# Joining attention items over heads and groups, and silu through tanh, in a hybrid decoder trunk

## The chip, the cores and the metric

The kernel runs on one core of one Trainium2 chip. The core has five engines that run their own instruction lists in order: TensorE (PE, matrix products, with its weight loads shown as PEld), VectorE (DVE), ScalarE (ACT), GpSimd (POOL) and SyncE (SP), which here only issues DMAs. The metric is the device time of one execution in microseconds (us), as the median of several runs; the kernel before took 1153.44 us (three runs, 1150.41 to 1153.8).

## The reference

One batch of 512 tokens, width 1024, goes through two layers. Layer 0 is a short gated convolution followed by a squared-ReLU MLP. Its output is normalised and projected once into a shared key and value side. Layer 1 is native sparse attention followed by another MLP. The part that matters here is the attention: 16 heads in 4 groups, head size 64, four query blocks of 128 tokens, a learned bias by distance, and three branches.

```python
# shared side, once
k_raw, v_raw, k_sel, v_sel, k_win, v_win = split(h @ w_kv)
k_cmp = silu(blocks(k_raw + pe_k) @ phi_k_w1) @ phi_k_w2    # 31 blocks of 32 tokens, stride 16
v_cmp = silu(blocks(v_raw + pe_v) @ phi_v_w1) @ phi_v_w2
# per query block and head
o_c = softmax(q k_cmp + bias) v_cmp        # compressed
o_s = softmax(q k_sel + bias) v_sel        # selected blocks: 16 of 8, so all causal ones
o_w = softmax(q k_win + bias) v_win        # window of 512: all causal keys
o   = gate0 * o_c + gate1 * o_s + gate2 * o_w
x   = x + o @ w_o
```

With 512 tokens there are 8 selection blocks and up to 16 may be chosen, so the second and third branch both run over all earlier keys.

## The kernel before

All matrix operands are split into a high and a low float16 part, and each product is three matmuls (`mm3`, L338 to L341: high by high, high by low, low by high). Weights come from HBM in pieces through SP's queue (`load_piece`, L147) and are split by ScalarE (`whi`) and VectorE (`wlo`) in `convert_piece` (L169), a few pieces ahead of use.

The attention stage lies in the block that starts at L598. First come the projections that every item needs (keys, values, gates, the queries of group 0; L860). Then two kinds of work are interleaved.

*Items* (L898 and L972). A `Full` item is one head of one group `g`, one query block `qb` and one branch `br`; it sees nk = 128, 256, 384 or 512 keys for qb 0 to 3. There are 128 of them. A `Cmp` item is the compressed branch of four heads of one group and one query block; there are 16. Each item has five steps, which are emitted for different items in one turn of the loop:
- st0: two logits matmuls into a bank "b" (two banks), a reduction on VectorE that adds the bias T and finds the maximum (L919), and the exponential on ScalarE, with a read of its sum (L922).
- st1, two items later: transposes of the probabilities into a bank "c" (two banks), copied to float16 as `at_ph` by ScalarE (L931).
- st2, three items later: VectorE forms the low part `at_pl` (L934).
- st3, four items later: three value matmuls per 128 keys into the bank "d" (L946 to L948). After the last head of a block VectorE scales by gate over sum, and GpSimd adds the parts of the three branches into the tile `o`.
- st4, six items later: `finish` (L879) transposes the finished output and splits it for the output projection.

A `Cmp` item does the same with plain additions, maxima and sums of VectorE (L990 to L1000), in tiles of its own (`c_s`, `c_p`, `c_ph`, `c_pl`).

*Background* (L1047) is a generator of matrix products that yields after every few matmuls: the raw compressed keys, the queries of group 1, `phi(0)` (the MLP of the compressed keys, with the silu at L793), the raw compressed values, `phi(1)`, the queries of groups 2 and 3, and, once groups 0 and 1 are done, the first half of the output projection. A turn of the loop gives it 1.7 yields for the first 64 items and 0.9 after (L1083); a yield is usually three matmuls. An item whose queries or compressed keys are missing forces the background on (L1071).

The order of items is set at L1045: full items of groups 0 and 1, compressed items of 0 and 1, full items of 2, compressed items of 2 and 3, full items of 3. Inside these rules the program's scheduler puts each engine's instructions into their final order, so that the lists differ a little from the order in which they are written. The bias tiles T (two buffers) are loaded by a DMA on ScalarE's queue (`load_T`, L619), a VectorE copy `Tc` of each sixteenth column behind it; the second half of a group's items starts the load for the next group.

## Time and profile before

| | us or share |
|---|---|
| median of the runs | 1153.44 |
| the profiled execution | 1151.28, its span 1149.5 |
| PE busy | 1106.0 (96%) |
| DVE busy | 837.8 (73%) |
| ACT busy | 582.7 (51%) |
| POOL busy | 162.2 (14%) |
| HBM over the span | 98 GB/s |

The profile is taken from one execution. A busy share counts the time between an instruction's start and end; TensorE's matmuls overlap, so that its share says little about how fast it could go. A row of a group of instructions has line, engine, operation, output and inputs, shape and count, then the busy time and the mean nanoseconds of one, then the idle time of the engine just before them with what ended it. A row of a table of windows has the stretch, its length, the busy time of each engine with its instructions in brackets, the share of TensorE's full clock, and the DMA engines' share and rate. A row of the timeline has start, length, engine, line, operation and shape.

### The profile page before, as it was taken

Reading aid. Unit: us, or ns where it says so; the run is one execution under the profiler, and the core shown is the slowest. Engines: PE = TensorE matmul, PEld = TensorE weight load, DVE = VectorE, ACT = ScalarE, POOL = GpSimd, SP = SyncE. Lnnn points to the kernel's source line nnn. Section 1 sums busy time; section 2 is a strip of 40 time slices with the busy share of each in tenths; the row PEclk is TensorE's granted clock in tenths of the full one; section 3 lists DMA queues with packets and bytes.
Section 4 is the critical chain, followed back from the end, with each engine's and each line's share of the span. In section 5 each row is a group of like instructions: output and inputs, shape, how many; then the busy total and the mean of one; then the engine's idle time right before and its main releaser. Section 6 shows DMA issues by size and latency. Waiting matters only on the chain.

```text
span 1149.5 us, 20386 instructions
## 1 busy us (share of the span) xinstructions
PE 1106.0 (96%) x7959; PEld 694.1 (60%) x7959; DVE 837.8 (73%) x1604; ACT 582.7 (51%) x983; POOL 162.2 (14%) x211
## 2 busy tenths in 40 slices
PE   9999999999999999999999899999999999999996
PEld 4444444447884458868466665765444688445885
DVE  4755557765897557988487898997985588754795
ACT  4523235345333444457679778676644534343452
POOL 0000000422000220000120023111132200022031
PEclk9999999999999999999999999999999999999998
DMA  6433235433433333314333530111643343330231
GB/s 208 130 92 110 92 111 174 119 93 93 127 98 108 109 110 107 97 55 122 110 79 99 143 94 19 57 38 38 186 126 99 88 126 110 104 99 19 75 92 74
DMA packets 149379, 115.76 MB, mean 101 GB/s; under 512 B 8612, under 2 KB 146564, under 8 KB 149284
## 3 DMA queue, kind: packets, MB, share of 16 engines
q1 hardware_dynamic: 146736, 109.47, 31.8%
q10 hardware_dynamic: 2260, 4.40, 1.3%
q8 instruction: 62, 1.02, 0.4%
q0 software_dynamic: 288, 0.61, 0.2%
q14 instruction: 33, 0.27, 0.1%
HBM read 110.22 MB, written 2.14 MB: 98 GB/s over the span
## 4 chain that ended last, share of the span: by engine, by line
PE 49%; DVE 20%; ACT 12%; issue 8%; POOL 6%; DMA 4%; SPq 0%; DVEq 0%; ACTq 0%; POOLq 0%
POOL ml_z L501 6%; PE a L340 4%; PE a L339 4%; PE a L341 4%; DVE wlo L183 4%; DMA wst<-mlp_w_dram 4%; ACT rh L502 3%; PE b L339 3%; PE b L340 3%; PE b L341 3%; PE c L341 3%; PE c L339 3%; PE c L340 3%; DVE wst L180 3%; DVE wlo L194 3%
## 5 line engine op out<-in xcount | busy, mean ns | idle before, releaser
L193 ACT ACTIVATE whi<-wst 128x1024 f16<-128x1024 f32 (+2 forms) x171 | 142.2, 857 | 128.3 <-PE b L340 40.0
L194 DVE SCALAR_TENSOR_TENSOR wlo<-wst,whi 128x1024 f16<-128x1024 f32 (+2 forms) x171 | 168.1, 990 | 47.3 <-ACT whi L193 47.1
L501 POOL TENSOR_TENSOR ml_z<-ml_z 128x256 f32<-128x256 f32 x128 | 101.1, 811 | 604.5 <-ACT ml_z L499 403.9
L182 ACT ACTIVATE whi<-wst 128x1792 f16<-128x1792 f32 x64 | 107.0, 1692 | 132.6 <-DVE wst L180 107.8
L341 PEld LDWEIGHTS <-wlo 128*128 128x128 f16 x1024 | 100.1, 98 | 109.3 <-DVE wlo L194 0.7
L339 PEld LDWEIGHTS <-whi 128*128 128x128 f16 x1024 | 100.4, 98 | 108.1 <-issue 3.7
L503 DVE TENSOR_TENSOR rl<-ml_z,rh 128x1792 f16<-128x1792 f32 x32 | 64.8, 2025 | 136.9 <-ACT rh L502 136.9
L340 PEld LDWEIGHTS <-whi 128*128 128x128 f16 x1024 | 100.2, 98 | 105.0 <-issue 1.7
L183 DVE SCALAR_TENSOR_TENSOR wlo<-wst,whi 128x1792 f16<-128x1792 f32 x64 | 129.8, 2033 | 3.6 <-ACT whi L182 3.6
L180 DVE TENSOR_TENSOR wst<-wst 128x256 f32<-128x256 f32 x256 | 105.9, 455 | 24.1 <-DMA wst<-mlp_w_dram 23.1
L502 ACT ACTIVATE rh<-ml_z 128x1792 f16<-128x1792 f32 x32 | 54.3, 1697 | 103.4 <-POOL ml_z L501 103.4
L550 PEld LDWEIGHTS <-wlo 128*128 128x128 f16 x896 | 88.1, 98 | 16.6 <-issue 5.1
L549 PEld LDWEIGHTS <-whi 128*128 128x128 f16 x896 | 88.1, 98 | 14.8 <-issue 3.9
L548 PEld LDWEIGHTS <-whi 128*128 128x128 f16 x896 | 88.2, 98 | 11.0
L499 ACT ACTIVATE ml_z<-ml_t 128x1024 f32<-128x1024 f32 x32 | 33.8, 1057 | 90.5 <-DVE ml_t L497 90.5
L341 PE MATMUL b<-xsh,wlo 128*128 128x512 f16 x208 | 78.8, 379 | 0.0
L340 PE MATMUL b<-xsl,whi 128*128 128x512 f16 x208 | 78.8, 379 | 0.0
L339 PE MATMUL b<-xsh,whi 128*128 128x512 f16 x208 | 78.7, 379 | 0.0
L922 ACT ACTIVATE at_p<-at_s,at_m 128x128 f32<-128x128 f32 (+3 forms) x128 | 71.3, 557 | 13.4 <-DVE at_m L919 13.0
L549 PE MATMUL a<-rl,whi 128*128 128x256 f16 x256 | 70.3, 275 | 4.6 <-DVE rl L503 4.6
L339 PE MATMUL c<-xsh,whi 128*128 128x512 f16 x192 | 72.8, 379 | 0.0
L340 PE MATMUL c<-xsl,whi 128*128 128x512 f16 x192 | 72.8, 379 | 0.0
(312 smaller groups left out, 2757.5 us busy)
## 6 DMA issues: line engine op xcount, KB each, us to landing
wst<-mlp_w_dram SPq DMA_DIRECT2D x256, 256.0 KB, 3.4
wst<-a_w_in_dram SPq DMA_DIRECT2D x18, 512.0 KB, 3.6
wst<-w_kv_dram SPq DMA_DIRECT2D x12, 512.0 KB, 3.7
T<-ext_d ACTq DMA_DIRECT2D x4, 1056.0 KB, 6.0
wst<-a_w_out_dram SPq DMA_DIRECT2D x8, 512.0 KB, 3.5
wst<-b_w_qg_dram SPq DMA_DIRECT2D x8, 512.0 KB, 4.3
wst<-b_w_o_dram SPq DMA_DIRECT2D x8, 512.0 KB, 3.5
wst<-a_w_in_dram SPq DMA_DIRECT2D x8, 384.0 KB, 5.5
```

The costliest lines, as they stand in the source:

```text
L180: DVE.tensor_tensor(b[:, :, o], b[:, :, x], b[:, :, y], op=e)
L182: ACT.activation(hi, b[:, :, 1:], AF.Copy, scale=sc)
L183: DVE.scalar_tensor_tensor(lo, b[:, :, 1:], sc, hi, op0=OP.mult, op1=OP.subtract)
L193: ACT.activation(hi[:, s:e], w, AF.Copy, scale=sc)
L194: DVE.scalar_tensor_tensor(lo[:, s:e], w, sc, hi[:, s:e], op0=OP.mult, op1=OP.subtract)
L339: PE.matmul(ps, w[0], xs[0], start=start, stop=False)
L340: PE.matmul(ps, w[0], xs[1], start=False, stop=False)
L341: PE.matmul(ps, w[1], xs[0], start=False, stop=stop)
L501: POOL.tensor_tensor(z[:, o], z[:, a], z[:, b], op=e)
L502: ACT.activation(rh[0][:, p], z[:, 1:8], AF.Copy)
L548: PE.matmul(acc7[i], wh, xh, start=c == 0 and not other, stop=False, skip_group_check=other)
L549: PE.matmul(acc7[i], wh, xl, start=False, stop=False, skip_group_check=other)
```

## The change

- A `Full` item now takes a tuple of heads: all four for query block 0, two for block 1, one for blocks 2 and 3, so that each item fills at most 512 columns. Logits, reductions and exponentials stay per head; transposes, the copy `at_ph`, the subtraction `at_pl` and the value matmuls run over the joined tile. 128 items become 88.
- A `Cmp` item takes the eight heads of two groups; its tiles come from `at_s`, `at_p`, `at_ph` and `at_pl`. 16 items become 8. `finish` can take two groups, and `add_parts` replaces the two places that add branches. The output tile `o` has six buffers, each for a pair of groups and one query block.
- The silu of `phi` is computed as v (1 + tanh(v/2)) / 2: the bias is copied twice, ScalarE applies tanh and adds one, VectorE multiplies.
- The background's yields now say what they cost, in us of TensorE (0.65, 0.33, 0.42, by default 0.1), and a turn gives 1.1 up to item 44 and 0.7 after; a wait for the output of groups 0 and 1 drops the credit.
- The loads of T for groups 1, 2 and 3 stand at items 11, 35 and 60; `Tc` is one tile for two groups. Tiles `vc_t` and `phi_hd` become `at_s` and `kr_hl`.

```diff
@@ load_T
-            c = ap.tile([128, 4, 32], F32, name="Tc", bufs=4)
-            DVE.tensor_copy(c, t[:, :, 0:512:16])
-            TC[g] = c
+            if g % 2 == 0:
+                TC[g // 2] = ap.tile([128, 2, 4, 32], F32, name="Tc", bufs=2)
+            DVE.tensor_copy(TC[g // 2][:, g % 2], t[:, :, 0:512:16])
@@ gated_pair (values: 0.33, phi: 0.42, out_proj: 0.65)
-                        yield
+                        yield 0.65
@@ phi
-                bcol = ap.tile([128, 1], F32, name="phi_b", bufs=2)
-                ACT.activation(bcol, ph[m][:, 124:125], AF.Copy, scale=1.0 / (SW * SK))
+                bias = ap.tile([128, 2], F32, name="phi_b", bufs=2)
+                ACT.activation(bias[:, 0:1], ph[m][:, 124:125], AF.Copy)
+                ACT.activation(bias[:, 1:2], ph[m][:, 124:125], AF.Copy, scale=0.5 / (SW * SK))
                 t = ap.tile([128, G, 31], F32, name="phi_t", bufs=2)
-                ACT.activation(t, ph[m][:, 0:124].rearrange("p (g j) -> p g j", g=4), AF.Silu,
-                               bias=bcol, scale=1.0 / (SW * SK))
-                split_to(hs[:, m, 0, :, 0:31], hs[:, m, 1, :, 0:31], t, SR)
+                v = ph[m][:, 0:124].rearrange("p (g j) -> p g j", g=4)
+                ACT.activation(t, v, AF.Tanh, bias=bias[:, 1:2], scale=0.5 / (SW * SK))
+                ACT.activation(t, t, AF.Identity, bias=ones)
+                DVE.scalar_tensor_tensor(t, v, bias[:, 0:1], t, op0=OP.add, op1=OP.mult)
+                split_to(hs[:, m, 0, :, 0:31], hs[:, m, 1, :, 0:31], t, 0.5 * SR / (SW * SK))
@@ add_parts, in place of add_part
+        def add_parts(g, n, qb, src, scale):
+            if (g // 2, qb) not in og:
+                og[g // 2, qb] = ap.tile([128, 2, 256], F32, name="o", bufs=6)
+            dst = og[g // 2, qb][:, g % 2:g % 2 + n].rearrange("p g (h d) -> p (g h) d", d=64)
...
+            t = ap.tile([128, 512], F32, name="o_t", bufs=1)[:, 0:nb * nh * 64].rearrange(
+                "p (b h d) -> p b h d", b=nb, d=64)
+            DVE.tensor_tensor(flat(t), flat(src), sc, op=OP.mult)
...
@@ Full.st0
-                q = Qs[g][:, h, qb * 128:(qb + 1) * 128]
-                PE.matmul(s[:, :nk], q, KD[:, br, 0, g, :nk], start=True, stop=False)
-                PE.matmul(s[:, :nk], q, KD[:, br, 1, g, :nk], start=False, stop=True)
+                for j, h in enumerate(self.heads):
+                    q = Qs[g][:, h, qb * 128:(qb + 1) * 128]
+                    o = s[:, j * nk:(j + 1) * nk]
+                    PE.matmul(o, q, KD[:, br, 0, g, :nk], start=True, stop=False)
+                    PE.matmul(o, q, KD[:, br, 1, g, :nk], start=False, stop=True)
...
+                for j, h in enumerate(self.heads):
+                    w = slice(j * nk, (j + 1) * nk)
+                    DVE.tensor_tensor_reduce(lg[:, w], s[:, w], TG[g][:, h, lo:lo - nk:-1], -1.0 / SL, 3e38,
+                                             OP.add, OP.min, mn[:, j:j + 1])
+                    ACT.activation(self.p[:, w], lg[:, w], AF.Exp, bias=mn[:, j:j + 1], scale=-1.0,
+                                   accum_out=l[:, br * 4 + h:br * 4 + h + 1])
@@ Full.st1, st2 (self.w = nk * len(heads))
-                for b in range(self.nb):
+                for b in range(self.w // 128):
                     PE.transpose(pt[:, b * 128:(b + 1) * 128], self.p[:, b * 128:(b + 1) * 128], ident)
-                ACT.activation(self.pt[0][:, :self.nk], self.ps, AF.Copy, scale=SP)
+                ACT.activation(self.pt[0], self.ps, AF.Copy, scale=SP)
@@ Cmp.st0
-                s = bank("b")[:, 0:128].rearrange("p (h n) -> p h n", h=4)
-                for h in range(4):
+                s = bank("b")[:, 0:256].rearrange("p (h n) -> p h n", h=8)
+                for j in range(8):
+                    g, h = 2 * gp + j // 4, j % 4
...
-                lg = ap.tile([128, 4, 32], F32, name="c_s", bufs=2)
+                lg = ftile("at_s", 3)[:, 0:256].rearrange("p (h n) -> p h n", h=8)
@@ items and loop
+        def heads_of(qb):
+            n = max(1, 4 >> qb) if qb < 2 else 1
+            return [tuple(range(h, h + n)) for h in range(0, 4, n)]
...
-        items = full(0) + full(1) + cmps(0) + cmps(1) + full(2) + cmps(2) + cmps(3) + full(3)
+        items = full(0) + full(1) + [Cmp(0, qb) for qb in range(4)] + full(2) + [Cmp(1, qb) for qb in range(4)]
+        items += full(3)
+        at_item = {11: lambda: load_T(1), 35: lambda: load_T(2), 60: lambda: load_T(3)}
...
-            credit += 1.7 if i < 64 else 0.9
-            while credit >= 1.0:
-                run_bg(1)
-                credit -= 1.0
+            credit += 1.1 if i < 44 else 0.7
+            while credit > 0.0:
+                u = next(bg, "end")
+                if u in ("wait", "end"):
+                    credit = 0.0
+                else:
+                    credit -= u or 0.1
```

More of the change, by code (lines that the diff above doesn't have):

```diff
@@ L701, in values @@
                     next(cv, None)
-                    yield
+                    yield 0.33
             drain(cv)
@@ L1007, in st1 @@
+                self.pt = [ap.tile([128, S], F16, name=n, bufs=3)[:, :self.w] for n in ("at_ph", "at_pl")]
+                self.ps = pt[:, :self.w]
                 ACT.activation(self.pt[0], self.ps, AF.Copy, scale=SP)
@@ L1012, in st3 @@
             def st3(self):
-                g, qb = self.g, self.qb
-                po = bank("e")[:, 0:256]
-                vc = [VC[:, i, g].rearrange("p h d -> p (h d)") for i in range(2)]
-                PE.matmul(po, self.pt[0], vc[0], start=True, stop=False)
-                PE.matmul(po, self.pt[0], vc[1], start=False, stop=False)
-                PE.matmul(po, self.pt[1], vc[0], start=False, stop=True)
-                rl = ap.tile([128, 4], F32, name="rlc", bufs=2)
+                g, qb, br = self.g, self.qb, self.br
@@ new lines, in st3 @@
+                k = keep[self.g, self.qb]
+                if k[0] is None:
+                    k[0] = bank("d")
+                vc = slice(br * 256 + g * 64, br * 256 + g * 64 + 64)
+                for j, h in enumerate(self.heads):
+                    o = k[0][:, (br * 4 + h) * 64:(br * 4 + h) * 64 + 64]
+                    for b in range(self.nb):
+                        at = j * self.nk + b * 128
+                        ph, pl = (u[:, at:at + 128] for u in self.pt)
+                        PE.matmul(o, ph, VT[:, b, 0, vc], start=b == 0, stop=False)
+                        PE.matmul(o, ph, VT[:, b, 1, vc], start=False, stop=False)
+                        PE.matmul(o, pl, VT[:, b, 0, vc], start=False, stop=b == self.nb - 1)
@@ new lines, in st3 @@
+                if self.heads[-1] == 3 and br == 1:
+                    rl = ap.tile([128, 8], F32, name="rl", bufs=2)
+                    by = rl.rearrange("p (b h) -> p b h", h=4)
+                    gt = GT[:, qb, 12 * g:12 * g + 12].rearrange("p (h b) -> p b h", b=3)[:, 1:3]
+                    DVE.reciprocal(rl, k[1])
+                    DVE.tensor_tensor(by, by, gt, op=OP.mult)
+                    add_parts(g, 1, qb, k[0].rearrange("p (b h d) -> p b h d", b=2, d=64), rl)
+                    self.last = parts[g, qb] == 2
+                else:
+                    self.last = False
@@ L1059, in body @@
         bg = background()
-        def run_bg(n):
-            for _ in range(n):
-                if next(bg, "end") in ("wait", "end"):
-                    return
         lead = {1: 2, 2: 3, 3: 4, 4: 6}
```

243 lines of the change are left out of this document (108 added, 135 removed).

## The prediction

> **What bounds the kernel now.** I read the busy shares by stage first, then the spacing of TensorE's instructions, then the groups of instructions. The attention items run from 559.5 to 796 us; before and after them TensorE is dense and the change issues nothing. The windows below cut that stage at the first item of each group (0, 1, then the compressed items of 0 and 1, group 2, compressed items of 2 and 3, group 3).
>
> ```profile
> span 1149.5 us, 20386 instructions
> ```
> ```profile
> core 0: us, PE busy (x) PEld busy (x) DVE busy (x) ACT busy (x) POOL busy (x), PEclk, DMA share, GB/s
> 559.50:613.90 54.40, 50.24 (x515) 34.54 (x514) 42.34 (x126) 42.84 (x115) 10.33 (x10) 1.00 0.32 90
> 613.90:676.30 62.40, 56.48 (x606) 37.79 (x605) 50.08 (x153) 51.06 (x142) 3.31 (x4) 1.00 0.37 104
> 676.30:691.10 14.80, 13.98 (x172) 9.28 (x171) 13.72 (x56) 8.83 (x23) 8.06 (x12) 1.00 0.38 112
> 691.10:735.60 44.50, 41.68 (x420) 27.86 (x418) 41.31 (x141) 36.20 (x112) 11.00 (x14) 1.00 0.12 37
> 735.60:748.60 13.00, 12.93 (x167) 9.06 (x165) 12.50 (x57) 6.93 (x21) 3.37 (x7) 1.00 0.14 42
> 748.60:796.00 47.40, 42.99 (x460) 29.39 (x461) 41.91 (x143) 34.93 (x110) 6.74 (x10) 1.00 0.12 35
> ```
>
> The stage takes 236.5 us. VectorE (DVE) sums to 201.9 in it and ScalarE (ACT) to 180.8, so neither is full. TensorE shows 218.3, but its records overlap, and what it needs is read from the spacing in a dense stretch of the timeline:
>
> ```profile
> 605.31 0.23 PE L341 MATMUL a<-big,wlo 128*128 128x155 f16 x1
> 605.38 0.60 PE L928 MATMUL c<-ident,at_p 128*128 128x128 f32 x4
> 605.82 0.19 PE L946 MATMUL d<-VT,at_ph 128*128 128x64 f16 x1
> ...
> 606.08 0.38 PE L914 MATMUL b<-KD,Q 128*128 128x512 f16 x1
> 606.30 0.38 PE L915 MATMUL b<-KD,Q 128*128 128x512 f16 x1
> ```
>
> A matmul of 155 columns takes 0.07 us, four transposes 0.44, the nine value matmuls between 605.82 and 606.08 take 0.029 each, one of 512 columns 0.216 (0.42 ns a column). The counts in the stage, grouped by shape:
>
> ```profile
> L928 PE MATMUL c<-ident,at_p 128*128 128x128 f32 x320 | 57.4, 279 | 6.1 <-DVE at_pl L934 5.4 <-ACT at_ph L931 0.2
> L946 PE MATMUL d<-VT,at_ph 128*128 128x64 f16 x320 | 43.5, 193 | 2.0 <-ACT at_ph L931 1.4 <-DVE o_t L957 0.3
> L341 PE MATMUL a<-xqh,wlo 128*128 128x512 f16 x48 | 18.2, 379 | 0.0
> L341 PE MATMUL a<-big,wlo 128*128 128x512 f16 x36 | 13.6, 379 | 0.0
> L341 PE MATMUL a<-big,wlo 128*128 128x155 f16 x64 | 13.6, 233 | 0.0
> L341 PE MATMUL a<-xsh,wlo 128*128 128x512 f16 x30 | 11.4, 379 | 0.0
> ```
>
> Each L341 stands for three matmuls. Background of 512 columns: 114 rows here and about 5 more, x3 x0.216 = 77; of 155 columns 64x3x0.07 = 13; transposes 320x0.11 = 35; value matmuls 3x320x0.029 = 28; logits, 32 items of each of four widths, two matmuls each, 64x(0.054+0.108+0.162+0.216) = 35; compressed items and final transposes about 14. Together some 203 us. So **TensorE's own work is 203 of the 236.5 us and bounds the stage; about 33 us are waits** for VectorE and ScalarE, mostly shorter than a record's tail and hence not all visible as idle time.
>
> Where are they? A full-attention item costs TensorE 0.31, 0.61, 0.91 or 1.22 us (query block 0 to 3). Next are the items (the reductions of L919, two records each) and then the background triples (L341) in three stretches:
>
> ```profile
> 632.10:648.20 16.10, 5.93 (x24) 1.00 0.57 152
> 691.10:708.60 17.50, 5.41 (x33) 1.00 0.11 32
> 776.80:787.80 11.00, 4.79 (x15) 1.00 0.17 49
> ```
> ```profile
> 632.10:648.20 16.10, 0.00 (x0) 0.00 (x0) 1.00 0.57 152
> 691.10:708.60 17.50, 3.39 (x9) 0.78 (x8) 1.00 0.11 32
> 776.80:787.80 11.00, 0.76 (x2) 0.20 (x2) 1.00 0.17 49
> ```
>
> First: 4 items of block 1 and 8 of block 2 need 9.7 us of TensorE and took 16.1, no background: 6.4 lost. Second: 8+8 small items 7.4, nine triples 5.9, transposes of finished outputs about 1.3: 2.9 lost. Third: seven items of block 3 8.5 and two triples 1.3: 1.2 lost, a pace of 1.57 us an item. **An item without background beside it runs at the pace of the VectorE/ScalarE handoffs, one with it at TensorE's.** These three hold 10.5 of the 33; the other 23 are spread, with the start of the stage and its last output among them.
>
> **The change part by part.** TensorE's work does not change: the same matmuls and transposes, in 96 items for 144.
>
> Joined full items. 32 copies and 32 subtractions of 128 columns become 8 of each at 512; 32 of 256 become 16 at 512. Reductions and exponentials stay one per head.
>
> ```profile
> L934 DVE SCALAR_TENSOR_TENSOR at_pl<-c,at_ph 128x128 f16<-128x128 f32 x32 | 8.9, 284 | 1.8 <-ACT at_ph L931 1.7
> L934 DVE SCALAR_TENSOR_TENSOR at_pl<-c,at_ph 128x256 f16<-128x256 f32 x32 | 13.2, 419 | 2.4 <-ACT at_ph L931 2.3
> L934 DVE SCALAR_TENSOR_TENSOR at_pl<-c,at_ph 128x512 f16<-128x512 f32 x32 | 21.8, 685 | 1.8 <-ACT at_ph L931 1.5
> L931 ACT ACTIVATE at_ph<-c 128x128 f16<-128x128 f32 x32 | 8.7, 273 | 2.1 <-PE c L928 1.9
> L931 ACT ACTIVATE at_ph<-c 128x256 f16<-128x256 f32 x32 | 12.0, 379 | 6.6 <-PE c L928 4.9 <-PE d L948 1.5
> L931 ACT ACTIVATE at_ph<-c 128x512 f16<-128x512 f32 x32 | 18.7, 586 | 5.9 <-PE c L928 5.8
> ```
>
> VectorE: 32x(0.284+0.419) = 22.5 becomes 24x0.685 = 16.4, 6.1 less. ScalarE: 20.9 becomes 14.1, 6.8 less.
>
> Compressed items, 16 to 8, each with twice the columns. A doubled instruction costs about 1.5 single ones (0.284 to 0.419), so two become one at a saving of a quarter. The two stretches of compressed items hold 13.72+12.50 = 26.2 us of VectorE, so about 6 less; ScalarE, a copy and an exponential an item, 2 less. Tiles at_s, at_p, at_ph now serve these items and the value conversion too, three buffers each: a wait could arise there. It holds at most the next item in the queue; I take it as nothing, since an item's at_s is free once its exponential has read it; the bound is one pace, 1.57, for each of 8 items, 12.6.
>
> Silu through tanh. Today each silu has its own table and the next exponential loads its own back:
>
> ```profile
> 656.20 1.28 ACT L793 ACT_TABLE_LOAD   x1
> 657.50 0.36 ACT L793 ACTIVATE phi_t<-a,phi_b 128x124 f32<-128x124 f32 x1
> ```
> ```profile
> L922 ACT ACT_TABLE_LOAD x4 | 5.1, 1283 | 0.1
> L793 ACT ACT_TABLE_LOAD x3 | 3.8, 1283 | 0.1
> ```
>
> In the changed program's ScalarE list one load is left in the stage: 6x1.28 = 7.7 us less. Added are four more bias copies, four adds of one and four VectorE multiplications, all 124 columns or fewer: at most 0.36 each by the L793 row, under 3 us on ScalarE, 1.4 on VectorE. [...]
>
> So VectorE goes from 202 to about 191 and ScalarE from 181 to about 167. None of it shortens TensorE's 203; it is worth only what it takes off the 33 us of waits.
>
> Background. Each item now brings 1.1 us of background up to item 44 and 0.7 after, by its TensorE cost and not by count. For the joined blocks that is 1.1 us beside 1.22 us of item, for 0.31 to 0.61 before. The built program's order of TensorE shows where it lands. Without background stand: three items of block 1 at the head of group 1; the last nine of group 1 (one of block 2, eight of block 3), then the drain of the last of them, then the 96 matmuls of 155 columns in one piece; the last four of group 3. Group 2 has two to six background matmuls beside nearly every item. Cost: at the 1.57 pace against 1.22, nine items lose 3.1; the drain waits for a copy and a subtraction, 0.586+0.685, 1.3; three joined items lose about 0.5 each, since two reductions and a subtraction on VectorE (some 1.7 us) stand against 1.22, 1.5; the last four 1.4. That is 7.3 for 10.5: **3 us less**.
>
> The other 23 us come from handoffs. Two thirds of the items are left and both serving engines carry 6 to 8% less. Between waits that scale with load (23x0.07 = 1.6) and with items (23x0.33 = 7.7) I take 5: a joined item has one copy-subtract handoff instead of four or two, but its four exponentials still stand in the ScalarE queue ahead of the next copy. **Sum: 8 us less**, bounds 4.6 to 10.7 by these rows alone; below that, the buffer wait of 12.6 turns it into 5 to 8 more.
>
> The bias table's load (T) is issued at items 11, 35 and 60, at least nine items before its group; it lands in 6 us by the row below, nine items take over 9. It costs nothing; if it came late, the copy to Tc would hold VectorE's queue and with it every reduction.
>
> ```profile
> T<-ext_d ACTq DMA_DIRECT2D x4, 1056.0 KB, 6.0
> ```
>
> The profiled execution took 1151.28 us around its span of 1149.5, 2.2 below the runs' median of 1153.44. 1151.3-8 = 1143.3; for a median I add half that offset: **1144.5**.
>
> **The rivals.**
> (a) *The waits do scale with handoffs and the joined items hide fully behind their background.* Waits fall from 33 to about 19: 14 less, 1139. For it: group 2's 44.5 us against 40 of need, now covered. Against: ScalarE still does four exponentials and their reads per joined item.
> (b) *Nothing measurable.* The stage is TensorE's 203 plus waits that move: the block of 155-column matmuls and the rest of the q2 projection run while VectorE and ScalarE idle for some 10 us, and they make that up in groups 2 and 3, where VectorE is already at 41.3 of 44.5. 1150 to 1155. Against: even idle for 10 and then at the 0.93 of group 2, VectorE needs 191/0.93+10 = 215.
> (c) *Slower: the joined item's longer chain is exposed.* TensorE's value matmuls wait for copy and subtraction of all heads: (586-273)+(685-284) = 0.71 us longer on 8 items, (586-379)+(685-419) = 0.47 on 16, 13.3 in all, and a bank of logits is held until the last head's reduction. With the 3 us of cover still gained it ends at +10, 1162; it turns slower once over 60% of the 13.3 is exposed with nothing won on the handoffs. For it: TensorE already waits 5.4 us for at_pl (L928 row). Against: 1.1 us of background and another item's 1.22 now lie between.
> (d) [...] One row shows a lowered clock:
>
> ```profile
> 900.00:1000.00 100.00, 97.16 (x754) 75.03 (x753) 79.05 (x126) 38.48 (x29) 7.37 (x11) 0.97 0.37 111
> ```
>
> Three in a hundred of the clock are lost over these 100 us, 3 us. The stage's windows all have 1.00. [...]
> (e) *That the change doesn't do what it says:* excluded for the loads and the joins, which stand in the built instruction lists.
>
> **How the numbers follow.** Forecast 0.42 (with (d), which shares its time, 0.47), (a) 0.17, (b) 0.16, (c) 0.20. About 0.3%, 3.5 us, is what a measurement of this kernel can tell from no change. Faster is forecast, (d) and (a): 0.64; same (b) 0.16; slower (c) 0.20. The likeliest case alone spans 1140 to 1149; the range takes half of (a), all of (b) and the near part of (c): 1135 to 1158.
>
> **What would show it.** In the changed profile the stage should last about 228 us, with group 2 near 41 and group 1 about as long as now; TensorE's need still 203; VectorE near 191, ScalarE near 167; one table load. Waits of the transposes for at_pl should fall below their 5.4 us. A stage under 224 speaks for (a). If group 2 does not shorten, cover was not what it lacked. If the value matmuls' waits (L946 to L948 now) for at_ph or at_pl in blocks 0 and 1 grow to several us, (c) holds. A clock below 1.00 in the stage would be (d). A first item of any group waiting for POOL's part of Q or for T would be a step that I left out.

## The result and the profile after

| | median | lowest to highest | runs |
|---|---|---|---|
| before | 1152.80 us | 1150.41 to 1157.10 | 6 |
| after | 1143.95 us | 1143.17 to 1147.34 | 6 |

The ratio is 0.9925, with a 95% interval from 0.9903 to 0.9948. The changed kernel is 8.85 us faster; 1144.5 us was forecast.

The profiled execution of the changed kernel is its longest, 1147.34 us at a granted clock of 0.987; its five other executions had 0.992 to 0.994, and the profiled one of the kernel before had 0.994. So a second profiled execution of the same kernel, of 1143.29 us at 0.994, stands beside it below, called the second profile. The page of the first begins:

```profile
span 1145.5 us, 20148 instructions
## 1 busy us (share of the span) xinstructions
PE 1102.9 (96%) x7959; PEld 695.8 (61%) x7959; DVE 833.8 (73%) x1504; ACT 569.7 (50%) x925; POOL 152.8 (13%) x201
```

These are its stage windows, cut as in the prediction (groups 0 and 1, the compressed items of both, group 2, the compressed items of 2 and 3, group 3):

```profile
core 0: us, PE busy (x) PEld busy (x) DVE busy (x) ACT busy (x) POOL busy (x), PEclk, DMA share, GB/s
559.00:612.90 53.90, 50.22 (x483) 33.71 (x483) 41.58 (x115) 39.62 (x104) 10.25 (x10) 0.94 0.24 66
612.90:676.00 63.10, 55.99 (x655) 40.67 (x654) 50.81 (x146) 44.66 (x131) 3.18 (x5) 0.97 0.41 115
676.00:691.60 15.60, 12.38 (x135) 7.59 (x134) 12.86 (x37) 8.38 (x19) 6.33 (x8) 0.96 0.43 138
691.60:735.00 43.40, 41.90 (x432) 29.55 (x430) 38.25 (x114) 35.27 (x97) 12.33 (x12) 0.98 0.12 38
735.00:743.20 8.20, 8.20 (x145) 6.55 (x142) 8.14 (x29) 4.47 (x12) 0.50 (x3) 1.00 0.21 66
743.20:791.00 47.80, 46.34 (x492) 32.14 (x490) 43.18 (x133) 35.00 (x101) 10.31 (x14) 1.00 0.12 35
sum 232.00, PE 215.02 PEld 150.21 DVE 194.83 ACT 167.39 POOL 42.88; mean PE 35.84 PEld 25.03 DVE 32.47 ACT 27.90 POOL 7.15
```

The stage takes 232.0 us for 236.5, with four clocks under 1.00 where all were 1.00. VectorE sums to 194.8 (201.9 before), ScalarE to 167.4 (180.8). What TensorE waits for longest in the stage, by the view of waits (total, times, longest):

```profile
PE b L937 <- POOL Q L739: 5.8, 9, 1.0
PE c L953 <- DVE at_pl L959: 4.0, 4, 1.8
PE a L339 <- DVE phi_t L798: 1.8, 1, 1.8
```

In the kernel before POOL's part of Q stood fourth in this list:

```profile
PE b L914 <- POOL Q L739: 1.9, 3, 0.9
```

The transposes' wait for at_pl went from 5.4 us to 4.0. New at the top is POOL's part of Q; 2.4 of its 5.8 us lie at the head of group 2, where the kernel before had none. One table load is left:

```profile
L947 ACT ACT_TABLE_LOAD x1 | 1.3, 1283 | 0.0
```

Busy windows hide waits shorter than a record's tail (those above call 215.0 of 232.0 us busy, the first profile's row below leaves 200.7 of 232.5 without its waits), so I worked out the waits from the trace itself: for every TensorE instruction the time to the start of the next one, less the lower quartile of that time over all instructions of its form. Time at half clock counts as a wait here. Each entry is the length of a stretch with its wait in brackets, in us; stretches begin at the first logits of groups 0 and 1, of the first compressed items, of group 2, of the second compressed items and of group 3, and end at the last transpose of an output. The rows below the first three are the experiments that follow.

```
                  group 0     group 1     comp. 0,1  group 2     comp. 2,3  group 3    stage  wait
before            54.3( 6.3)  61.6(11.4)  12.1(0.6)  48.0( 7.6)  10.0(0.2)  50.8(9.1)  236.8  35.3
after             51.9( 7.2)  65.3(12.6)  11.8(2.0)  47.4( 6.4)   6.9(0.0)  49.2(3.5)  232.5  31.8
after, 2nd        49.4( 4.9)  65.3(12.8)  11.8(2.0)  47.5( 6.7)   6.9(0.0)  49.2(3.6)  230.2  30.0
silu              51.9( 7.3)  65.6(13.2)  12.1(2.0)  46.8( 5.9)   6.9(0.0)  49.2(3.5)  232.6  31.9
tanh_only         55.6( 7.6)  61.6(11.4)  12.1(0.5)  48.0( 7.6)  10.0(0.2)  50.9(9.2)  238.1  36.6
single_heads      51.0( 6.4)  66.8(14.1)  11.8(2.0)  49.6( 8.7)   6.9(0.0)  53.4(7.7)  239.5  38.9
split_full        50.6( 6.0)  64.9(12.2)  11.8(2.0)  48.1( 7.1)   6.9(0.0)  50.8(4.8)  233.1  32.1
cmp_own           51.1( 6.5)  64.0(11.3)  17.7(6.9)  46.4( 6.5)   9.2(0.9)  51.6(7.3)  240.1  39.4
split_cmp         49.4( 4.8)  64.2(11.5)  13.5(3.6)  46.8( 5.9)   6.9(0.0)  50.9(5.2)  231.6  31.0
cmp_cover         49.4( 4.9)  65.6(13.0)  17.8(6.9)  46.1( 6.4)  10.7(0.6)  48.9(5.7)  238.6  37.5
old_cover         51.8( 5.9)  65.4(14.9)  12.5(1.6)  49.6(11.2)   8.2(0.0)  48.5(3.2)  235.9  36.9
credit            54.3( 6.3)  66.4(11.0)   7.1(0.2)  43.0( 4.5)   6.9(0.0)  48.8(5.1)  226.5  27.1
q2_first          49.4( 4.8)  59.9( 4.5)  12.2(1.8)  47.9( 7.6)   6.9(0.0)  48.4(4.7)  224.8  23.3
```

Stage less wait, TensorE's own need, is 201.5 us before, 200.2 in the second profile, and between 199 and 202 in every row. From before to the second profile the span falls by 8.0, the stage by 6.6, and 5.3 of these are waits. By groups most of that is group 3, whose waits fall by 5.5; group 1 waits 1.4 longer than before. Cut further, at the first logits of each query block, the waits of blocks 0 to 2 fall by some 12 us over the four groups, and those of block 3 grow by some 6, from 9.2 to 15.2: block 3 of group 1 alone goes from 2.0 us to 10.2, of which up to 1.7 are half clock.

### The profile page after: what moved, and what is told of

Its sections match the earlier page's. It is cut to its first block, busy times and chain, and to the rows that moved or that the text cites. A ratio compares the mean times of both kernels' runs of the same rounds, so it can differ in the third digit from the quotient of the medians.

```text
span 1145.5 us, 20148 instructions
## 1 busy us (share of the span) xinstructions
PE 1102.9 (96%) x7959; PEld 695.8 (61%) x7959; DVE 833.8 (73%) x1504; ACT 569.7 (50%) x925; POOL 152.8 (13%) x201
## 4 chain that ended last, share of the span: by engine, by line
PE 58%; DVE 17%; ACT 8%; issue 6%; POOL 5%; DMA 4%; SPq 0%; DVEq 0%; ACTq 0%; POOLq 0%
PE a L339 5%; PE a L340 5%; PE a L341 5%; POOL ml_z L501 4%; DMA wst<-mlp_w_dram 4%; PE c L341 3%; PE c L339 3%; PE c L340 3%; PE b L340 3%; PE b L339 3%; DVE wlo L183 3%; PE b L341 3%; ACT rh L502 3%; PE c L953 2%; DVE wlo L194 2%
## 5 line engine op out<-in xcount | busy, mean ns | idle before, releaser
L501 POOL TENSOR_TENSOR ml_z<-ml_z 128x256 f32<-128x256 f32 x128 | 95.7, 769 | 609.7 <-ACT ml_z L499 607.1
L180 DVE TENSOR_TENSOR wst<-wst 128x256 f32<-128x256 f32 x256 | 110.1, 473 | 28.0 <-DMA wst<-mlp_w_dram 27.0
L341 PE MATMUL c<-xsh,wlo 128*128 128x512 f16 x192 | 73.5, 383 | 0.0
```

The lines of the kernel that those rows point to most:

```text
L180: DVE.tensor_tensor(b[:, :, o], b[:, :, x], b[:, :, y], op=e)
L341: PE.matmul(ps, w[1], xs[0], start=False, stop=stop)
L501: POOL.tensor_tensor(z[:, o], z[:, a], z[:, b], op=e)
```

## The experiments

Each was timed against the kernel before on the same chip. The runs were spread over three chips, on which the kernel before had medians from 1152.73 to 1154.37 us, so a difference of a microsecond or two between the medians of two runs says little; the ratios are the safer measure. "again" is the changed kernel once more.

| run | median us | ratio to before, 95% interval | mean clock, runs |
|---|---|---|---|
| again | 1144.47 | 0.9920 (0.9896 to 0.9943) | 0.9935, 6 |
| silu | 1147.41 | 0.9948 (0.9925 to 0.9971) | 0.9916, 7 |
| tanh_only | 1154.23 | 1.0001 (0.9988 to 1.0014) | 0.9928, 12 |
| single_heads | 1153.58 | 0.9998 (0.9984 to 1.0013) | 0.9934, 12 |
| split_full | 1146.32 | 0.9940 (0.9924 to 0.9955) | 0.9920, 6 |
| cmp_single | 1154.70 | 1.0004 (0.9989 to 1.0018) | 0.9912, 12 |
| cmp_own | 1154.00 | 1.0008 (0.9995 to 1.0021) | 0.9912, 12 |
| split_cmp | 1147.89 | 0.9954 (0.9939 to 0.9970) | 0.9922, 6 |
| cmp_cover | 1153.78 | 0.9995 (0.9980 to 1.0011) | 0.9908, 12 |
| old_cover | 1151.86 | 1.0002 (0.9984 to 1.0020) | 0.9893, 12 |
| credit | 1145.15 | 0.9924 (0.9908 to 0.9940) | 0.9940, 6 |
| q2_first | 1143.43 | 0.9913 (0.9896 to 0.9930) | 0.9935, 6 |

### The changed kernel again

No edit.

> The changed kernel once more, beside the others on one chip. Theory (fewer handoffs, and background beside the items of blocks 0 and 1): 1143 to 1145 us, 8 to 9.5 below the kernel before, and a profile in which the stage from 559 us on takes about 229 us, since the execution profiled first lost some 3 us to three stretches at half clock. Rival (those half-clock stretches belong to the change, being its own pauses): they stand at the same places again and the stage takes 232.

The stage took 230.2 us and the median is 1144.47. Two half-clock stretches stand at the places of the first profile, 2 us earlier in the span (from 643.83 and 688.21 us, for 645.83 and 690.20); the one of group 0 is missing. So the rival holds for two of the three: they belong to loose spots of this kernel but do not all come every time. Rows of the first profile, then of the second:

```profile
560.50:567.30 6.80, 6.11 (x22) 2.90 (x23) 3.21 (x21) 3.88 (x19) 1.59 (x2) 0.50 0.24 77
645.80:649.20 3.40, 3.03 (x17) 1.62 (x17) 3.40 (x10) 2.06 (x6) 0.00 (x0) 0.50 0.43 94
690.20:693.60 3.40, 3.18 (x18) 2.16 (x19) 1.78 (x16) 1.09 (x5) 2.36 (x2) 0.50 0.02 5
```
```profile
643.83:647.25 3.42, 3.21 (x18) 1.85 (x18) 3.13 (x8) 1.90 (x5) 0.00 (x0) 0.50 0.51 111
688.21:691.62 3.41, 2.94 (x16) 1.80 (x14) 1.90 (x17) 1.37 (x6) 2.10 (x2) 0.50 0.02 5
```

### Silu and tanh

Silu put back into the changed kernel:

```diff
...
-                ACT.activation(t, v, AF.Tanh, bias=bias[:, 1:2], scale=0.5 / (SW * SK))
-                ACT.activation(t, t, AF.Identity, bias=ones)
-                DVE.scalar_tensor_tensor(t, v, bias[:, 0:1], t, op0=OP.add, op1=OP.mult)
+                ACT.activation(t, ph[m][:, 0:124].rearrange("p (g j) -> p g j", g=4), AF.Silu,
+                               bias=bcol, scale=1.0 / (SW * SK))
...
```

> The changed kernel with the table of silu put back, joins as they are. By table loads of 1.28 us, three of them silu's and three to get back to the exponential, ScalarE gets 7.7 us more, less 3 for the copies and adds that go. Theory: nearly all of it lies beside TensorE's work, since only the block of 155-column matmuls stands around them: 0 to 2 us more than the changed kernel. Rival 1 (ScalarE sets the pace of the uncovered items): 4 to 5 us more. Rival 2 (the tanh chain's extra steps, which hold bank a until the multiplication, cost more than the loads): 0.5 to 2 us less than the changed kernel.

The reverse: tanh alone, in the kernel before.

> The kernel before with tanh alone in place of silu. Putting silu back into the changed kernel cost 2.9 us. Theory (the loads' 7.7 us of ScalarE lie partly beside TensorE's work, in either kernel): 1 to 3 us below the kernel before. Rival (in the kernel before other waits take the place, so that tanh pays only beside the joins): within 1 us of it.

Alone, tanh is worth nothing that can be measured: the rival of the second run. With the joins, putting silu back cost 2.9 us by the medians, with intervals that overlap: between the theory's 0 to 2 and the first rival's 4 to 5. Group 0's 2.5 us in the table are a half-clock stretch ahead of the first silu, which the first profile of the changed kernel has too. The five other stretches sum to 180.6 us here and 180.7 in the second profile, but that one lost up to 3.4 of them to half clock (its rows above, half of 3.42 + 3.41) and this one's clock was 1.00 there. So in the stage the loads cost between nothing and some 3.4 of their 7.7 us; a closer figure, and whether silu brings a lower mean clock with it, stays open.

### One head to an item again, and joined items with split copies

Blocks 0 and 1 with one head to an item, the background per block as in the changed kernel:

```diff
-            n = max(1, 4 >> qb) if qb < 2 else 1
+            n = 1
...
-            credit += 1.1 if i < 44 else 0.7
+                share = 0.25 if g_of < 9 and it.qb == 0 else 0.5 if g_of < 9 and it.qb == 1 else 1.0
...
+            credit += (1.1 if g_of < 2 else 0.7) * share
```

> The changed kernel with one head to an item in the full-attention blocks 0 and 1, compressed items and tanh as they are; the background's share per block is kept (a quarter of 1.1 or 0.7 us per item of block 0, half per item of block 1), so that only the handoffs change. VectorE gets 6.1 us and ScalarE 6.8 us more by the rows of the copy and the subtraction. Theory (the items' handoffs cost TensorE its waits): 3 to 5 us more than the changed kernel, the loss in the stretches of blocks 0 and 1 of every group. Rival 1 (it is where the background lies, not the join): within 1 us of the changed kernel. Rival 2 (the joined item's longer chain is exposed): faster than the changed kernel by 2 or more.

It lost the whole gain, 9.1 us for 3 to 5 expected. In the table the waits grow by 1.5, 1.3, 2.0 and 4.1 us in groups 0 to 3, and nowhere else. Cut by query blocks it is where the small ones are: blocks 0 and 1 of the four groups wait some 10 us longer, blocks 2 and 3 some 2 less (a half-clock stretch, worth up to 1.7, lies in block 3 of group 1 in the second profile and in block 0 of group 0 here). In the groups of instructions, cut to the stage, the transposes (L953) and the value matmuls (L972) show it. First the second profile, then this run:

```profile
L953 PE MATMUL c<-ident,at_p 128*128 128x128 f32 x320 | 51.3, 277 | 4.2 <-DVE at_pl L959 4.1
L972 PE MATMUL d<-VT,at_ph 128*128 128x64 f16 x320 | 38.9, 194 | 0.6 <-DVE o_t L890 0.5
```
```profile
L953 PE MATMUL c<-ident,at_p 128*128 128x128 f32 x320 | 57.3, 278 | 8.0 <-DVE at_pl L959 7.7 <-DVE big L362 0.2
L972 PE MATMUL d<-VT,at_ph 128*128 128x64 f16 x320 | 42.6, 194 | 2.3 <-ACT at_ph L956 1.4 <-DVE o_t L890 0.5
```

Is it the fixed costs of 40 more copies and 40 more subtractions? The next kernel keeps the joined items and cuts only these two instructions per head:

```diff
-                ACT.activation(self.pt[0], self.ps, AF.Copy, scale=SP)
+                for w in self.each():
+                    ACT.activation(self.pt[0][:, w], self.ps[:, w], AF.Copy, scale=SP)
...
-                DVE.scalar_tensor_tensor(self.pt[1], self.ps, SP, self.pt[0], op0=OP.mult, op1=OP.subtract)
+                for w in self.each():
+                    DVE.scalar_tensor_tensor(self.pt[1][:, w], self.ps[:, w], SP, self.pt[0][:, w],
+                                             op0=OP.mult, op1=OP.subtract)
```

> The changed kernel, items joined as they are and in the same order, but with the copy and the subtraction of each joined item cut back to one per head: VectorE and ScalarE get their 6.1 and 6.8 us again, while the distance between an item's stages on TensorE (two to six items, so 1.2 us of matmuls apiece in a joined block and 0.3 to 0.6 with one head) stays the joined one. With one head to an item the kernel lost 9.1 us of 8.9 gained. Theory A (fixed costs of the instructions on VectorE and ScalarE): 6 to 9 us more than the changed kernel. Theory B (the stages of small items follow each other too closely, and the join moves them apart): 0 to 2 us more.

1146.32 us, 1.9 more than "again", with intervals of the ratios that overlap: theory B. So of the 9.1 the fixed costs of the two instructions are about 2. The other 7 go with the number of items: with one head to an item, the next stage of an item follows two to six small items later instead of as many joined ones, and each item has a quarter or half of the background beside it.

### The compressed items

One group to an item, 16 for 8, half the background to each; first in the changed kernel's shared tiles, then in tiles of their own as before the change:

```diff
-        items = full(0) + full(1) + [Cmp(0, qb) for qb in range(4)] + full(2) + [Cmp(1, qb) for qb in range(4)]
+        items = full(0) + full(1) + [Cmp(0, qb, j) for j in range(2) for qb in range(4)] + full(2)
+        items += [Cmp(1, qb, j) for j in range(2) for qb in range(4)]
...
+            credit += 1.1 if i < 44 else 0.35 if i < len(items) and isinstance(items[i], Cmp) else 0.7
```

> The changed kernel with compressed items of one group each, 16 for 8, half the background's share per item, so that the background per stretch stays the same. VectorE gets about 6 us and ScalarE 2 us more. The first trace has 8.2 us for the second stretch of compressed items against 13.0 before the change, and 15.6 for the first against 14.8. Theory (VectorE sets the pace of the second stretch): 3 to 5 us more than the changed kernel, all in the second stretch, nothing in the first. Rival (the second stretch was shorter since its background had moved elsewhere): within 1 us.

> Compressed items of one group each, as in the run that came out at 1154.7 us, but in tiles of their own again (as in the kernel before), instead of the three buffers that they share with the full items and with the value conversion of the projections. Theory A (one group per item costs VectorE's and ScalarE's fixed costs): 1151 to 1155 us as there. Theory B (in that run the sixteen items queued for the shared buffers; the join itself is worth little): 1145 to 1148 us, with the first stretch of compressed items near 12 us again instead of 18.

Both lose everything, where the first run's theory had 3 to 5 us, none of it in the first stretch. The shared buffers are not it: the first stretch takes 18.0 us in them and still 17.7 in tiles of their own, for 11.8 in the second profile. Windows of that stretch in the second profile, then in the run with its own tiles:

```profile
673.20:685.00 11.80, 10.45 (x134) 6.82 (x132) 11.51 (x35) 8.31 (x21) 2.23 (x4) 1.00 0.57 183
```
```profile
673.70:691.40 17.70, 14.83 (x144) 8.70 (x142) 15.62 (x69) 10.46 (x30) 4.77 (x9) 0.84 0.36 122
```

VectorE is busy 11.51 of 11.80 us with 35 instructions there and 15.62 of 17.70 with 69: it is the fullest engine of the stretch in both, and the clock of 0.84 takes up to 0.16x17.7 = 2.8 us of the 5.9 that are lost. The kernel before, with sixteen items too, has in the first compressed stretch and in group 2:

```profile
675.10:687.20 12.10, 12.01 (x166) 8.01 (x163) 11.02 (x44) 8.46 (x21) 4.47 (x8) 1.00 0.56 172
687.20:735.20 48.00, 44.45 (x432) 29.53 (x431) 44.81 (x156) 37.17 (x117) 14.58 (x19) 1.00 0.11 35
```

There TensorE is full in the first stretch, and VectorE's work (44 instructions only) is done in group 2 at 44.81 of 48.00. I read this so: where TensorE has independent work to go on with, VectorE's backlog is put off and comes due later. It was not tried by itself.

The next kernel cuts only the instructions of the joined items, one for each group again (add, maximum, subtraction, exponential, sum, copy, low part, scaling and the addition into `o`):

```diff
-                DVE.tensor_reduce(mx, lg[:, :, :n], axis=mybir.AxisListType.X, op=OP.max)
+                for u in two:
...
+                    DVE.tensor_reduce(mx[:, u], lg[:, u, :n], axis=mybir.AxisListType.X, op=OP.max)
```

> The changed kernel, compressed items joined over two groups, but each of their instructions on VectorE and ScalarE cut into one for each group again; order, tiles and background as in the changed kernel. Sixteen single items cost 10 us more than eight joined ones, of which the trace shows 5.9 us in the first stretch of compressed items, 2.3 in the second and 2.4 in group 3 behind it. Theory A (these stretches and the head of group 3 run at VectorE's pace, so its fixed costs count): 4 to 8 us more than the changed kernel. Theory B (as with the full items, it is the distance between the stages, not VectorE's work): 0 to 2 us more.

1147.89 us, 3.4 more than "again", a little under theory A's 4. The first stretch grows by 1.7 and group 3 by 1.7; a half-clock stretch at 683.24 us, inside the first, takes up to 1.2 of its part. So here the fixed costs are about a third, perhaps less, and the rest again goes with the number of items. Is it their cover?

```diff
-            credit += 1.1 if i < 44 else 0.35 if i < len(items) and isinstance(items[i], Cmp) else 0.7
+            credit += 1.1 if i < 44 else 0.7
```

> The kernel with compressed items of one group in tiles of their own (1154.0 us) with 0.7 us of background for each of them instead of 0.35, so that sixteen single items have as much cover apiece as the eight joined ones. The order of TensorE stays nearly the same in the first stretch of compressed items, where the rest of q for group 2 stands ahead of them either way, and changes in the second and in group 3: about 2.8 us of background move there from behind. Theory (what a join buys is cover per item: one background, fewer handoffs to share it): the 2.3 us of the second stretch and the 2.4 of group 3 come back, 1149 to 1151 us, while the first stretch keeps its 17.7 us. Rival (VectorE's extra work for single items sets their pace, covered or not): 1153 to 1155 us.

1153.78 us: the rival. The second compressed stretch and group 3 together went from 60.8 us to 59.6, where the joined items take 56.1. More background beside single compressed items brings 1.2 of 4.7 back; lack of cover is not the main thing that holds them there.

### The old sharing of the background

The joined items with the background given out by heads, as before the change:

```diff
-            credit += 1.1 if i < 44 else 0.7
+            it = items[min(i, len(items) - 1)]
+            heads = 2 if isinstance(it, Cmp) else len(it.heads)
+            credit += heads * (0.8 if i < 40 else 0.42)
```

> The changed kernel, items joined, but the background shared out as the kernel before did it, by the number of heads and not per item: 0.8 us a head up to the end of group 1 and 0.42 after (a compressed item counts as two), so that a joined item of four heads brings 3.2 us of it and one of block 3 only 0.8. The sum over all items is the same 85 us. Theory A (half of the gain comes from cover that moved from the small blocks to the large ones): 3 to 6 us more than the changed kernel, in the second half of each group. Theory B (the distance between the stages of joined items is all of it): within 1.5 us of the changed kernel.

The higher share ends at item 40, four items before group 1 does. Nothing is left of the gain here either, by the ratio of 1.0002; the median is 1151.86 us, 7.4 more than "again" for theory A's 3 to 6. The stage's waits are 36.9 us, 6.9 more than in the second profile, in groups 1 and 2, and the value matmuls come into the groups of instructions with waits for at_ph and for o_t:

```profile
L953 PE MATMUL c<-ident,at_p 128*128 128x128 f32 x320 | 51.5, 281 | 6.3 <-DVE at_pl L959 3.2 <-DVE rl L980 2.4 <-DVE big L362 0.2
L972 PE MATMUL d<-VT,at_ph 128*128 128x64 f16 x320 | 40.0, 194 | 4.8 <-ACT at_ph L956 3.2 <-DVE o_t L890 1.6
```

Part of it is the clock. Over twelve executions it averages 0.9893, the lowest of all kernels, and the profile has four half-clock stretches in the stage, two more than the second profile:

```profile
619.60:623.00 3.40, 3.40 (x13) 1.21 (x11) 3.15 (x10) 3.39 (x14) 0.00 (x0) 0.52 0.00 0
640.23:643.64 3.41, 3.41 (x31) 2.43 (x27) 3.41 (x10) 2.26 (x6) 0.00 (x0) 0.50 0.36 82
691.50:695.00 3.50, 2.92 (x15) 1.74 (x16) 2.03 (x18) 2.10 (x11) 1.79 (x2) 0.52 0.48 154
729.00:732.40 3.40, 3.12 (x16) 2.06 (x17) 3.04 (x8) 1.81 (x5) 0.72 (x1) 0.50 0.00 0
```

The product of span and clock averages 1139.0 us here, 1135.4 in "again" and 1144.0 in the kernel before on this chip (1145.0 on the chip of "again"): by this estimate half of the loss is clock, half plain waits.

### More background early, and the order of the background

The new wait for POOL's part of Q at the head of group 2 was a step that the prediction left out. Here are two ways to take it away: more background per item up to the end of group 1,

```diff
-            credit += 1.1 if i < 44 else 0.7
+            credit += 1.35 if i < 44 else 0.55
```

> The changed kernel with 1.35 us of background per item in groups 0 and 1 for 1.1, and 0.55 after for 0.7, so that the projection of q for group 2 is done before the first compressed items, not just ahead of group 2. Theory (the first items of group 2 stand behind POOL's part of that Q, 3.4 us of TensorE, and the projection behind at_s of VectorE, 0.9): 3 to 4.5 us less than the changed kernel, 1140 to 1141.5. Rival (the wait goes but groups 2 and 3 lose as much cover): within 1 us of it.

and the projection of q for group 2 ahead of the second phi (its weight pieces move with it, which is not shown):

```diff
             yield from raw(1)
-            yield from marked("cmp", phi(1))
             yield from marked("q2", queries(2))
+            yield from marked("cmp", phi(1))
```

> The changed kernel with the projection of q for group 2 ahead of the second phi in the background, its two weight pieces moved with it. In the changed kernel the last eleven items of group 1 stand alone from 639 to 657 us, since the next background, the 96 matmuls of 155 columns, waits for the copies of kr through its one kr_hl buffer; the wait there is some 8 us, the one of group 2's first items for POOL's part of Q 3.4, and the one for bank a at 664 us 2.0. Theory (these waits only lack independent work beside them): 6 to 10 us less than the changed kernel, 1134 to 1138. Rival (the work that is moved is missing between phi's multiplication and the compressed items, as with more background per item, which gained nothing): within 1.5 us of the changed kernel.

The first brought nothing, 1145.15 us: the rival. Its stage of 226.5 us is 3.7 below the second profile's, of which up to 3.4 are that one's half clock; the first compressed stretch fell by 4.7 us and group 2 by 4.5, and group 0 grew by 4.9, since the work moved there. In the second the profile shows what was meant. Group 1 falls from 65.3 us to 59.9, its wait from 12.8 to 4.5. In the second profile of the changed kernel the copies of kr went out in two batches, the second held back by the one kr_hl buffer, and the 96 matmuls began only when it had landed:

```profile
L763 SPq DMA_DIRECT2D big<-kr_hl x4: 591/604/615, 643.5 to 654.2; - x4
L765 SPq DMA_DIRECT2D big<-kr_hl x4: 593/602/607, 644.8 to 655.5; - x4
L360 ACT ACTIVATE kr_hl<-at_s x2: 620/626/631, 641.1 to 650.2; 128x512 f16<-128x512 f32 x2
DMA to landing us min/median/max: 1.9/2.3/2.9
```

(Columns of the first three: duration of the shortest, median and longest in ns, first and last start in us.) The last one starts at 655.5 and lands 1.9 to 2.9 us later; the first of the 96 starts at 657.45 (timeline of TensorE, after the last value matmul ahead of it):

```profile
656.59 0.19 PE L974 MATMUL d<-VT,at_pl 128*128 128x64 f16 x1
657.45 0.23 PE L339 MATMUL a<-big,whi 128*128 128x155 f16 x1 [0.66 <-issue]
```

With q's matmuls in that gap most of the waits are gone. Yet the median is 1143.43 us, 1.0 below "again" with overlapping intervals: within the rival's 1.5. In the profiled execution the stage is 5.4 us shorter (the changed kernel's half-clock stretches, at most 3.4 us, among it) and the rest after it 3.0 longer, 355.9 us for 352.9, with a half-clock stretch in it:

```profile
904.00:909.00 5.00, 4.31 (x25) 3.15 (x25) 4.50 (x3) 3.60 (x4) 0.00 (x0) 0.66 0.17 44
```

In the thirteen profiles of the table that rest lies between 352.1 and 356.5 us, a spread as large as most of the differences in the stage. Where the other executions lose it was not tried. It is the fastest median of the study, but not shown to beat the changed kernel.

## Why the prediction was right, and where not

**TensorE's need bounds the stage.** Right: 203 us forecast, 199 to 202 in thirteen profiles, whatever the edit. The matmuls are the same in all of them, so this says that the price of one was read rightly; the differences between the stages are nearly all waits.

**Sum and stage.** 8 us less were forecast, 8.85 came. The stage was to take 228 us; it took 230.2 in the second profile, of which half clock is at most half of 3.42+3.41, 3.4 by its two rows. VectorE came to 195 for 191, ScalarE to 167 for 167. That the sum fits this well is partly luck: neither of its two terms came where the working had put it, as the next two paragraphs show.

**"Uncovered stretches, 3 us less".** The place is wrong, and so is a price. The pace of 1.57 us for an item without background contains two triples: seven items of 1.22 lost 1.2 in their row, 0.17 each, so nine items would lose 1.5 and not 3.1. Measured, the end of group 1 costs far more than either: its items from 639 to 657 us wait 8.0 us in the second profile, up to 1.7 of them half clock, where nine items and the drain had 4.4. Group 1 was to stay; it grew by 3.7 us, 1.4 of it waits, the rest work. Group 2 was to fall to 41 and hardly moved (44.5 to 43.4 by the prediction's cuts, 48.0 to 47.5 by the first logits). Its first items wait for POOL's part of Q, and a half-clock stretch follows; the first was named as a step that might be left out, and it was. That these two are the reason is not shown: without both, group 2 takes 43.0 us in the run with more background early, but 47.9 with q's projection moved. What came instead is blocks 0 to 2, which wait some 12 us less, by groups above all group 3: waits of 9.1 us became 3.6.

**"Handoffs, 5 us less".** The sum treats cover and handoffs as two terms that add. The runs show they don't: single heads, single compressed items or the old sharing, each alone, lose 7 to 10 us by the medians, 9 to 10 by the ratios. The working priced the joins by VectorE's and ScalarE's loads and by the number of items; the split instructions show that the loads are about 2 us (full items) and 3.4 (compressed), and that the larger part goes with the number of items. What exactly it is about the items (their distance or their cover) is only shown in part: for joined full items cover decides (old_cover, half of whose loss is clock), for single compressed ones it mostly doesn't (cmp_cover). Distance alone was not varied.

**Costs taken as nothing.** The shared at_s, at_p and at_ph buffers, bounded by 12.6 us, cost nothing that shows: with sixteen single items, which use them more often, own tiles gave 0.7 us, within the spread. No wait for T appears among the longest. The working had not listed one wait of 1.8 us, the first matmul of q held by bank a until the tanh chain's multiplication. It is not the price of phi's extra instructions: with silu in the changed kernel the same matmul waits 1.7 us.

**The rivals.** (c) fell: the value matmuls wait 0.6 us (L972 above) and 0.5 (for at_pl) in the whole stage, not several. Its own turning point was off: with 3 us of cover gained and nothing on the handoffs it turns slower once 3 of the 13.3 are exposed, 23% and not 60%, which belongs to the full 8. (b) fell with the time. (a) did not come, nor did any of the twelve kernels reach its 1139 us as a median. (d), a clock below 1.00 in the stage, did come in the profiled executions: 0.50 in three stretches of the first profile and in two of the second. No pause over 2.2 us of TensorE, from one start to the next, stands ahead of the first profile's three. In the lowered row of the kernel before the half-clock stretch starts at 914.91 us, and the longest steps there from one start of TensorE to the next are 1.32 and 2.06 us (a second stretch at half clock is that kernel's end, from 1143.6 us). Over the executions of "again" the clock averages 0.9935, over those of the kernel before beside it 0.9936, so half clock cost the change nothing on balance.

## What to carry to other kernels

Give background by the item, that is by the handoff, and not by the amount of work in it: when items are joined, the sharing has to be changed with them, and the same join without it brought nothing that could be measured. Measure TensorE's waits from start to start, since the sum of its records called 218 of 236 us busy where 201 were needed. And when three edits each lose the whole gain if undone, don't price them one by one: look for the stretch in which their effects meet: here, as I read it, the small blocks and what VectorE still has to do when they begin.

## What the runs showed of the hardware

In the profiles of this case TensorE's granted clock stood at 0.50 for some microseconds at a time. In the first profile that is, within the stage, from 560.49 us for 6.83 us and from 645.83 and 690.20 us for 3.41 us each. These starts lie 25 and 13 times 3.413 us apart, and in every one of the fourteen profiles that has more than one such stretch the starts lie whole multiples of 3.413 us apart, from a place that differs between the profiles. What sets that step was not shown. These are the windows of 3.41 us just ahead of the three stretches:

```profile
557.08:560.49 3.41, 1.69 (x13) 0.62 (x11) 1.07 (x2) 3.32 (x5) 3.26 (x3) 1.00 0.02 5
642.41:645.83 3.42, 1.45 (x17) 0.88 (x16) 3.42 (x7) 1.71 (x5) 0.00 (x0) 1.00 0.00 0
686.79:690.20 3.41, 1.30 (x12) 0.64 (x13) 2.36 (x6) 1.05 (x2) 3.18 (x4) 1.00 0.00 0
```

TensorE's records cover 50%, 42% and 38% of them, and the longest steps from one start to the next there are 1.26, 2.20 and 1.40 us. So two or three short waits in one window stood ahead of half clock at these places. In the second profile windows counted back by 3.413 us from its stretch at 643.83 us cut the first of these places in two, of 74% and 59%, and the clock stayed at 1.00:

```profile
555.09:558.50 3.41, 2.52 (x13) 0.97 (x12) 1.94 (x3) 2.50 (x5) 1.22 (x2) 1.00 0.24 85
558.50:561.91 3.41, 2.00 (x16) 0.84 (x16) 1.67 (x1) 2.44 (x3) 3.26 (x3) 1.00 0.02 5
```

So the same loose spot stood ahead of 6.83 us at half clock, worth up to 3.4 us, in one execution and of none in the other. Over all fourteen profiles, counting windows of 3.413 us laid in the same way, at full clock and without the first and last microseconds, half clock followed all 32 windows in which the records cover less than 42%, 17 of the 96 between 42% and 61%, and none of the 4471 above that. These are counts of this case; what tells the 17 from the other 79, and whether the records' cover is what matters, was not measured.
